# A hybrid mLSTM and convolution block on one core: four contraction tiles in a row for one PSUM bank, where each bank took one in turn

## The chip, the cores and the metric

The kernel runs on one core of one Trainium2 chip, as one launch. The metric is the device time of one execution in microseconds (us), shown as the median of the runs of a kernel. The engines are TensorE (PE; its weight loads are a row of their own, PEld), VectorE (DVE), ScalarE (ACT), GpSimd (POOL) and SyncE (SP), which issues the transfers.

## What is computed

One encoder layer on 2048 tokens of width 1024, in float32, followed by a final RMSNorm. Cut to what matters:

```
u    = rmsnorm(x, norm_g)
proj = u @ w_in                       # 1024 -> 5*1024 + 8 + 3*1024 columns
q, k, v, o_pre, z_m, i_pre, f_pre, glu_a, glu_g, z_c = split(proj)
hm   = mlstm_chunkwise(q, k, v, i_pre + b, f_pre + b)       # 4 heads of 256
hm   = headwise_rmsnorm(sigmoid(o_pre) * hm) * mh_norm_g * silu(z_m)
c    = causal_depthwise_conv31(glu_a * sigmoid(glu_g)) + conv_b
c    = silu(layernorm(c)) * silu(z_c)
h    = x + concat(hm, c) @ w_out                            # 2048 -> 1024 columns
out  = rmsnorm(h, final_norm_g)
```

## The kernel before

The tokens are taken in two halves of 1024. Every large product is made of three fp32r products: a float32 operand is split into a high part and the rest (`uh`, `ul` for activations, `wh`, `wl` for weights), and `wh*uh + wh*ul + wl*uh` is summed in PSUM.

The work is cut into units (`unit`, line 315). A unit fills four PSUM banks, `ps[0]` to `ps[3]` (tiles `gm_<n>_0` to `gm_<n>_3`; n is the number of the unit's first weight tile), from the pool `gm`, which has five banks. It runs over the contraction in steps `kc`: 8 steps of 128 rows in the input projection, 16 in the output projection. `products(kc, i)` (line 321) issues the matmuls of one step into one bank: three of 512 columns, or six of 256, or three of 264. Lines 350 to 357 hold the order: the step is the outer loop, the bank the inner one, so a bank takes one contraction tile and then its neighbour takes the same one. After the last step, lines 361 to 368 hand each bank to `evac`, which reads it out on ACT and DVE with high priority; the next unit needs those banks again.

The units of one half are, in order: one GLU unit (`g`), the two units of v of head 0 with the gates (`v0`), another `g`; then for each of the four heads v (head 0 had its own), o, z, q, k and two `g` units; at last four units `c`. Then the next half, then eight units of the output projection (blocks `b` of 512 tokens, `nn` of 512 columns).

Weights come as a stream. `w_load` (line 193) fetches two tiles (`wr`) in one transfer, `w_prep_` (line 210) splits a tile: ACT casts it to `wh` (line 215), POOL subtracts to get `wl` (line 216). The pool `wp` holds four tiles of each kind, and `w_advance(i)` (line 221) asks for tiles up to i + 3. A weight tile covers two steps in the input projection and one in the output projection.

Beside the units run three streams: the mLSTM of the head just projected, cut into slots, one slot after each step (`ml_slot`, line 173); the convolution's 31 taps for each channel block and the layer norm, taken from a queue at a fixed rate (`pump`, line 138), with most of the work on DVE; and the loads of the next activations (`hook`). For each chunk of 128 tokens the mLSTM runs `s0` (scores `sk` on PE; weighted scores `w`, their split `wsh`, `wsl`; scaled queries split into `qssh`, `qssl`), two slots later `s1` (`num` on PE, out of those splits and the split state `c0h`, `c0l`, `c1h`, `c1l`), and then the transposes `mt`. A tile scheduler orders each engine's instructions by priority, the place in the program, and its own timeline; the order is then fixed, and each engine works through its own list in that order.

Of the kernel before, what the change touches and what calls it, by code (L numbers as in the profile page):

```python
# [19 lines left out]
P = 128  # L20
D = 1024            # model width
SEQ = 2048
HT = 1024           # tokens per half
NH = 4              # mLSTM heads
HD = 256            # head width
L = 128             # mLSTM chunk
NCH = HT // L       # chunks per half
NB = 8              # 128-channel blocks of the conv group
# [3 lines left out]
VW = HD + 2         # value row with the ones column (even width)  # L32

# columns of the per-feature vector pack
# [5 lines left out]
def hybrid_block_kernel(  # L40
    ctx: ExitStack,
    tc: tile.TileContext,
    x: bass.AP,        # [SEQ, D]
    xT: bass.AP,       # [2, 8, P, HT]
    wu: bass.AP,       # [NU, 2, P, 4, 256]
    wv0: bass.AP,      # [2, P, 4, 264]
    wo: bass.AP,       # [2, 8, P, 2, 512]
    vecs: bass.AP,     # [P, NVEC]
    bg: bass.AP,       # [1, 8]
    fg: bass.AP,       # [1, D]  # L50
    out: bass.AP,      # [1, SEQ, D]
):
# [3 lines left out]
    WARM = 16  # L56

# [5 lines left out]
    wp = pool("wp", 4)  # L63
# [17 lines left out]
    ones = cp.tile([P, P], F32, name="ones")  # L81
    nc.gpsimd.memset(ones, 1.0)
    # until the data arrive: load the first function table, wake the tensor engine
# [48 lines left out]
    def in_turn(ins):  # L132
        """the first of the background work after a pause stays behind what was emitted before it"""
        if pin[0]:
            tc.keep_in_program_order(ins)
            pin[0] = False
# [19 lines left out]
    # mLSTM work in slots, one per step of the products that it runs beside  # L156
# [30 lines left out]
    # every entry: (dram AP of two tiles [P, 2, n], n); tiles are prepared ahead  # L187
# [31 lines left out]
    WAHEAD = 3  # L219

    def w_advance(i):
        """make tiles up to i + WAHEAD ready (emission order)"""
# [9 lines left out]
    uh, ul = {}, {}  # L232

    # The reciprocal rms of a token scales its row of every product, so the
    # products start on x * norm_g and the factor is applied where they leave PSUM.
# [19 lines left out]
    def bcast_cols(cols, n, nm):  # L255
        """[P tokens, n] columns -> PSUM [P, n*128]: the values along the free dim on all partitions"""
# [56 lines left out]
    wpos = [0]  # L313

    def unit(kind, nk, kpt, ncol, opnd, evac, step_us=2.6, hook=None, toks=None, ntail=0):
        """nk steps over the contraction, kpt per weight tile of kpt*ncol columns;
        the last ntail steps run bank by bank"""
# [31 lines left out]
        tail = nk - ntail  # L349
        for kc in range(tail):  # L350
            w_advance(base + kc // kpt)
            if hook is not None:
                hook(kc)
            for i in range(4):
                products(kc, i)
            ml_slot()
            pump(step_us * PUMP)
        for kc in range(tail, nk):
            w_advance(base + kc // kpt)
        wpos[0] += nk // kpt  # L360
        for i in range(4):
            for kc in range(tail, nk):
                products(kc, i)
            if hook is not None:
                for kc in range(tail + i * ntail // 4, tail + (i + 1) * ntail // 4):
                    hook(kc)
            with first_hand():
                evac(i, ps[i])
# [752 lines left out]
```

## Time and profile before

| | |
|---|---|
| runs (us) | 2030.17, 2029.78, 2030.05 |
| median (us) | 2030.05 |
| profiled execution, span from the first to the last instruction (us) | 2027.0 |
| PE busy | 1997.0 us (99%), 11562 matmuls |
| DVE busy | 1431.9 us (71%) |
| ACT busy | 828.6 us (41%) |
| POOL busy | 803.1 us (40%) |
| mean granted TensorE clock | 0.993 of 2.4 GHz |

The profiled execution is shown with its span alone; the times of the runs are 2.8 to 3.2 us above it, which is what lies around a span. A busy PE is not a PE at its peak: matmuls overlap in the records, so the pace is read from the distance between starts. The granted clock is one of two levels, 1.00 (2.4 GHz) and 0.50 (1.2 GHz); a stretch that holds both shows a mean.

### The profile page before, as it was taken

How to read it: one execution, taken by the hardware profiler on the slowest of the kernel's cores; microseconds unless marked ns; L12 is line 12 of the kernel's file. 1: busy time of each engine (PE TensorE's matmuls, PEld its weight loads, DVE VectorE, ACT ScalarE, POOL GpSimd, SP SyncE). 2: the span in 40 equal slices, each digit the busy share in tenths (PEclk: the TensorE clock that was granted, in tenths of full speed). 3: DMA queues.
4: the chain of work that ended last, by engine and by line, in shares of the span. 5: the costliest groups of instructions: out<-in, count | busy, mean ns of one | idle time of the engine just before them, and what ended most of it. 6: DMA issues, size and time to landing. Idle time of an engine off the chain costs nothing. (4 is left out here: it accounts for less than half of the span.)

```text
span 2027.0 us, 29786 instructions
## 1 busy us (share of the span) xinstructions
PE 1997.0 (99%) x11562; PEld 1750.5 (86%) x11562; DVE 1431.9 (71%) x1915; ACT 828.6 (41%) x1703; POOL 803.1 (40%) x740
## 2 busy tenths in 40 slices
PE   9999999999999999999999999999999999999998
PEld 7998898899899888888789879988998888788886
DVE  5598887689588855646799998977895658733231
ACT  5233432443343255535445225424523555543332
POOL 4632432343343232534333423433422326556464
PEclk9999999999999999999999999999999999999999
DMA  4121121111122233335311211211221566766452
GB/s 150 63 68 53 57 67 50 63 48 63 53 68 65 82 110 104 121 107 164 106 56 43 68 52 58 74 53 52 68 69 53 161 222 206 266 206 232 151 182 94
DMA packets 85837, 204.11 MB, mean 101 GB/s; under 512 B 7296, under 2 KB 40256, under 8 KB 85696
## 3 DMA queue, kind: packets, MB, share of 16 engines
q1 hardware_dynamic: 85696, 202.21, 29.8%
q8 instruction: 91, 1.49, 0.3%
q14 instruction: 50, 0.41, 0.1%
HBM read 159.15 MB, written 43.03 MB: 100 GB/s over the span
## 5 line engine op out<-in xcount | busy, mean ns | idle before, releaser
L216 POOL TENSOR_TENSOR wl<-wr,wh 128x512 fp32r<-128x512 f32 (+1 forms) x392 | 611.3, 1564 | 858.6 <-ACT wh L215 832.1
L781 DVE SCALAR_TENSOR_TENSOR y<-c,vec,y 128x1024 f32<-128x1024 f32 x480 | 707.3, 1474 | 9.5
L330 PE MATMUL gm<-ul_u,wh 128*128 128x512 f32 x1280 | 506.0, 395 | 0.4 <-DVE ul_u L287 0.4
L330 PE MATMUL gm<-uh_u,wl 128*128 128x512 f32 x1280 | 501.6, 394 | 0.0
L330 PE MATMUL gm<-uh_u,wh 128*128 128x512 f32 x1280 | 499.7, 395 | 1.6 <-DVE oz L445 1.0
L215 ACT CAST wh<-wr 128x512 fp32r<-128x512 f32 (+1 forms) x392 | 241.3, 619 | 596.5 <-PE gm L330 214.2
L337 PE MATMUL gm<-wh,uh_u 128*128 128x256 f32 x1408 | 286.9, 283 | 5.5 <-DVE oz L445 3.4
L330 PEld LDWEIGHTS gm<-uh_u,wh 128*128 128x128 f32 x1280 | 240.7, 188 | 54.5 <-DVE oz L445 1.4
L337 PE MATMUL gm<-wh,ul_u 128*128 128x256 f32 x1408 | 286.9, 282 | 0.0
L330 PEld LDWEIGHTS gm<-ul_u,wh 128*128 128x128 f32 x1280 | 241.0, 188 | 51.4 <-DVE ul_u L287 1.1
L330 PEld LDWEIGHTS gm<-uh_u,wl 128*128 128x128 f32 x1280 | 240.9, 188 | 51.6 <-POOL wl L216 0.3
L337 PE MATMUL gm<-wl,uh_u 128*128 128x256 f32 x1408 | 283.7, 282 | 0.0
L337 PEld LDWEIGHTS gm<-wh,uh_u 128*128 128x128 f32 x1408 | 219.2, 190 | 7.2 <-DVE oz L445 3.6
L337 PEld LDWEIGHTS gm<-wh,ul_u 128*128 128x128 f32 x1408 | 219.2, 190 | 0.1
L337 PEld LDWEIGHTS gm<-wl,uh_u 128*128 128x128 f32 x1408 | 217.8, 190 | 0.1
L344 PE MATMUL gm<-wh,uh_m 128*128 128x512 f32 x512 | 202.2, 396 | 2.2 <-ACT wh L215 2.2
L344 PE MATMUL gm<-wh,ul_m 128*128 128x512 f32 x512 | 202.6, 396 | 0.0
L344 PE MATMUL gm<-wl,uh_m 128*128 128x512 f32 x512 | 199.3, 396 | 0.8 <-POOL wl L216 0.8
L344 PEld LDWEIGHTS gm<-wh,uh_m 128*128 128x128 f32 x512 | 96.6, 189 | 24.7 <-ACT wh L215 2.5
L344 PEld LDWEIGHTS gm<-wl,uh_m 128*128 128x128 f32 x512 | 96.5, 188 | 23.2 <-POOL wl L216 1.2
L344 PEld LDWEIGHTS gm<-wh,ul_m 128*128 128x128 f32 x512 | 96.5, 189 | 22.2
L694 POOL TENSOR_TENSOR ss<-ss,nhalf 128x1 f32<-128x1 f32 x64 | 54.7, 854 | 133.3 <-ACT sq L693 131.0
(216 smaller groups left out, 2390.2 us busy)
## 6 DMA issues: line engine op xcount, KB each, us to landing
wr<-in_wu SPq DMA_DIRECT2D x123, 512.0 KB, 3.5
wr<-in_wo SPq DMA_DIRECT2D x64, 512.0 KB, 3.5
mr<-mixs SPq DMA_DIRECT2D x32, 512.0 KB, 4.6
ysc<-y SPq DMA_DIRECT2D x16, 512.0 KB, 2.6
mixs<-mo SPq DMA_DIRECT2D x32, 256.0 KB, 2.1
zsc<-zc SPq DMA_DIRECT2D x32, 256.0 KB, 2.2
ly<-ysc SPq DMA_DIRECT2D x16, 512.0 KB, 4.7
lz<-zsc SPq DMA_DIRECT2D x16, 512.0 KB, 5.7
```

What stands on the lines that cost most here:

```text
L215: nc.scalar.copy(hi[:, :n], s)
L216: nc.gpsimd.tensor_tensor(out=lo[:, :n], in0=s, in1=hi[:, :n].bitcast(F32), op=ALU.subtract)
L330: nc.tensor.matmul(ps[i], wt[:, o + cb * P : o + (cb + 1) * P], at[:, tb * 512 : (tb + 1) * 512], start=st, stop=sp_,)
L337: nc.tensor.matmul(ps[i][:, t2 * 256 : (t2 + 1) * 256], at[:, t * P : (t + 1) * P], wt[:, o : o + ncol], start=st and t2 == 0, stop=sp_, s ...
L344: nc.tensor.matmul(ps[i][:, :ncol], at[:, t * P : (t + 1) * P], wt[:, o : o + ncol], start=st, stop=sp_,)
L694: nc.gpsimd.tensor_tensor(out=ss, in0=ss, in1=nhalf[:, 0:1], op=ALU.pow)
L781: tc.keep_in_program_order(nc.vector.scalar_tensor_tensor(out=y, in0=c[:, j + i * H2 : j + (i + 1) * H2], scalar=col(V_CW, b * CW + j), in1=y,
```

## The change

`unit` gets a parameter `grp`. The steps are cut into groups of `grp`; within a group the bank is the outer loop and the step the inner one, so that one bank takes `grp` contraction tiles in a row before the next bank does. Input-projection units use 4, but the first and the last unit of each half keep 1; output-projection units use 2. In the last group each bank is read out as soon as its own products are issued. The mLSTM slots and the pumped work keep their rate, one per step's worth of products: with a group of four, one after each bank. All weight tiles of a group are asked for at its start, and stay in use until its last bank; the pool keeps its four buffers (`NW = 4`). Line numbers move by one or two. Comments are removed as well.

```diff
-    wp = pool("wp", 4)
+    wp = pool("wp", NW)
...
-    WAHEAD = 3
+    WAHEAD = NW - 1
...
-    def unit(kind, nk, kpt, ncol, opnd, evac, step_us=2.6, hook=None, toks=None, ntail=0):
+    def unit(kind, nk, kpt, ncol, opnd, evac, step_us=2.6, hook=None, toks=None, ntail=0, grp=1):
...
-        tail = nk - ntail
-        for kc in range(tail):
-            w_advance(base + kc // kpt)
-            if hook is not None:
-                hook(kc)
-            for i in range(4):
-                products(kc, i)
+        def step():
             ml_slot()
             pump(step_us * PUMP)
-        for kc in range(tail, nk):
-            w_advance(base + kc // kpt)
-        wpos[0] += nk // kpt
-        for i in range(4):
-            for kc in range(tail, nk):
-                products(kc, i)
...
-            with first_hand():
-                evac(i, ps[i])
-            for _ in range(ntail // 4):
-                ml_slot()
-                pump(step_us * PUMP)
+        bounds = list(range(0, nk - ntail, grp)) + [nk - ntail] + ([nk] if ntail else [])
+        for lo, hi in zip(bounds, bounds[1:]):
+            for kc in range(lo, hi):
+                w_advance(base + kc // kpt)
+            if hi == nk:
+                wpos[0] += nk // kpt
+            for i in range(4):
+                cut = lambda j: lo + j * (hi - lo) // 4
...
+                for kc in range(lo, hi):
+                    products(kc, i)
+                if hi == nk:
+                    with first_hand():
+                        evac(i, ps[i])
+                for _ in range(cut(i + 1) - cut(i)):
+                    step()
...
+            grp = 1 if ui in (0, len(s) - 1) else 4
...
-                unit("fm", 8, 2, 256, opnd, ev_glu(hf, i), hook=hook)
+                unit("fm", 8, 2, 256, opnd, ev_glu(hf, i), hook=hook, grp=grp)
...
-                 ntail=4 if (b, nn) == (3, 1) else 0)
+                 ntail=4 if (b, nn) == (3, 1) else 0, grp=2)
```

How PE's order moves, at three places. First, inside the unit of q of head 3 in the first half (`gm_108`; the rows name bank, activation part and weight part). Before:

```order
L330 MATMUL gm_108_1_6870<-uh_u0_5_238,wh110_6798 128x512
L330 MATMUL gm_108_1_6870<-ul_u0_5_239,wh110_6798 128x512
L330 MATMUL gm_108_1_6870<-uh_u0_5_238,wl110_6799 128x512
L330 MATMUL gm_108_2_6871<-uh_u0_5_238,wh110_6798 128x512
L330 MATMUL gm_108_2_6871<-ul_u0_5_239,wh110_6798 128x512
L330 MATMUL gm_108_2_6871<-uh_u0_5_238,wl110_6799 128x512
L330 MATMUL gm_108_3_6872<-uh_u0_5_238,wh110_6798 128x512
L330 MATMUL gm_108_3_6872<-ul_u0_5_239,wh110_6798 128x512
L330 MATMUL gm_108_3_6872<-uh_u0_5_238,wl110_6799 128x512
```

And on PE in the same unit of the changed kernel, its second group:

```order
L331 MATMUL gm_108_0_6870<-uh_u0_4_230,wh110_6749 128x512
L331 MATMUL gm_108_0_6870<-ul_u0_4_231,wh110_6749 128x512
L331 MATMUL gm_108_0_6870<-uh_u0_4_230,wl110_6750 128x512
L331 MATMUL gm_108_0_6870<-uh_u0_5_238,wh110_6749 128x512
L331 MATMUL gm_108_0_6870<-ul_u0_5_239,wh110_6749 128x512
L331 MATMUL gm_108_0_6870<-uh_u0_5_238,wl110_6750 128x512
L331 MATMUL gm_108_0_6870<-uh_u0_6_246,wh111_6874 128x512
L331 MATMUL gm_108_0_6870<-ul_u0_6_247,wh111_6874 128x512
L331 MATMUL gm_108_0_6870<-uh_u0_6_246,wl111_6875 128x512
L331 MATMUL gm_108_0_6870<-uh_u0_7_254,wh111_6874 128x512
L331 MATMUL gm_108_0_6870<-ul_u0_7_255,wh111_6874 128x512
L331 MATMUL gm_108_0_6870<-uh_u0_7_254,wl111_6875 128x512
```

The bank changed after three products and now changes after twelve. Over the program PE's list has 2629 such stretches on one `gm` bank before and 1365 after, with the same 11356 matmul instructions.

Second, PE in the unit of z of head 0 in the second half (`gm_152`), where its fourth bank is first written. Before:

```order
L337 MATMUL gm_152_2_9322<-wh155_9324,uh_u1_7_8280 128x256 x2
L337 MATMUL gm_152_2_9322<-wh155_9324,ul_u1_7_8281 128x256 x2
L337 MATMUL gm_152_2_9322<-wl155_9325,uh_u1_7_8280 128x256 x2
L337 MATMUL gm_152_3_9323<-wh152_9118,uh_u1_0_8102 128x256 x2
L337 MATMUL gm_152_3_9323<-wh152_9118,ul_u1_0_8103 128x256 x2
L337 MATMUL gm_152_3_9323<-wl152_9119,uh_u1_0_8102 128x256 x2
```

In the changed kernel PE stands thus at the same point:

```order
L338 MATMUL gm_152_2_9322<-wl153_9181,uh_u1_3_8178 128x256
L338 MATMUL gm_152_0_9320<-wh154_9186,uh_u1_4_8198 128x256 x2
L338 MATMUL gm_152_0_9320<-wh154_9186,ul_u1_4_8199 128x256
L338 MATMUL gm_152_3_9323<-wh152_9044,uh_u1_0_8102 128x256 x2
L338 MATMUL gm_152_3_9323<-wh152_9044,ul_u1_0_8103 128x256 x2
L338 MATMUL gm_152_3_9323<-wl152_9045,uh_u1_0_8102 128x256 x2
```

Before, the scheduler ran the first three banks through all eight steps and left the whole of the fourth bank for the end; now the fourth bank starts after the first group, with the first products of bank 0's second group ahead of it.

Third, PE at the first chunk of the mLSTM of head 1 in the second half, beside the GLU unit `gm_192`. Before:

```order
L330 MATMUL gm_192_3_11740<-uh_u1_3_8178,wh193_11654 128x512
L330 MATMUL gm_192_3_11740<-ul_u1_3_8179,wh193_11654 128x512
L595 MATMUL num_1_1_0_11811<-v_1_1_0_10937,wsh_1_1_0_11768 128x258 x2
L595 MATMUL kv_1_1_0_0_11821<-v_1_1_0_10937,kw_1_1_0_11765 128x258 x3
L595 MATMUL num_1_1_0_11811<-v_1_1_0_10937,wsl_1_1_0_11769 128x258
L330 MATMUL gm_192_3_11740<-uh_u1_3_8178,wl193_11655 128x512
```

In the changed kernel these rows of PE read:

```order
L331 MATMUL gm_192_1_11743<-ul_u1_7_8281,wh195_11746 128x512
L331 MATMUL gm_192_1_11743<-uh_u1_7_8280,wl195_11747 128x512
L596 MATMUL num_1_1_0_11816<-v_1_1_0_10782,wsh_1_1_0_11779 128x258 x2
L596 MATMUL kv_1_1_0_0_11826<-v_1_1_0_10782,kw_1_1_0_11776 128x258
L596 MATMUL num_1_1_0_11816<-v_1_1_0_10782,wsl_1_1_0_11780 128x258
```

The chunk's last `sk` row stands 26 rows of 512 columns above `num` before and 60 such rows above it now. For the first chunk of head 0 in that half it is 29 rows before and 62 now. For some later chunks it goes the other way: chunk 7 of head 1 in the first half has 29 rows between `sk` and `num` before and 16 now.

## Rows read from the trace of the kernel before

**Rows 1.** The page's head: the span, and busy time of each engine.
```profile
span 2027.0 us, 29786 instructions
...
PE 1997.0 (99%) x11562; PEld 1750.5 (86%) x11562; DVE 1431.9 (71%) x1915; ACT 828.6 (41%) x1703; POOL 803.1 (40%) x740
```

**Rows 2.** What PE waited for: us in total, times, longest us.
```profile
PE num L595 <- DVE qssl L586: 4.0, 3, 2.5
PE gm L337 <- DVE oz L445: 3.4, 1, 3.4
PE us L247 <- DVE sm L296: 2.8, 1, 2.8
PE gm L344 <- ACT wh L215: 2.2, 1, 2.2
PE num L595 <- ACT wsh L585: 2.1, 1, 2.1
PE mt L708 <- DVE hm L700: 1.6, 1, 1.6
...
PE gm L337 <- ACT oz L432: 1.2, 2, 0.9
PE gm L330 <- DVE oz L445: 1.0, 1, 1.0
PE gm L344 <- POOL wl L216: 0.8, 1, 0.8
PE gm L337 <- DVE v L402: 0.8, 1, 0.8
```

**Rows 3.** PE's timeline in unit gm_164: start, us, engine, line, operation, tiles.
```profile
1005.13 0.39 PE L330 MATMUL gm<-uh_u,wl 128*128 128x512 f32 x1
1005.36 0.39 PE L330 MATMUL gm<-uh_u,wh 128*128 128x512 f32 x1
1005.59 0.39 PE L330 MATMUL gm<-ul_u,wh 128*128 128x512 f32 x1
1005.82 0.39 PE L330 MATMUL gm<-uh_u,wl 128*128 128x512 f32 x1
1006.04 0.39 PE L330 MATMUL gm<-uh_u,wh 128*128 128x512 f32 x1
1006.27 0.39 PE L330 MATMUL gm<-ul_u,wh 128*128 128x512 f32 x1
1006.50 0.39 PE L330 MATMUL gm<-uh_u,wl 128*128 128x512 f32 x1
```

**Rows 4.** PE's timeline in unit gm_152, around its fourth bank's first product.
```profile
936.02 0.40 PE L337 MATMUL gm<-wl,uh_u 128*128 128x256 f32 x2
939.85 0.80 PE L337 MATMUL gm<-wh,uh_u 128*128 128x256 f32 x2 [3.43 <-DVE oz L445]
940.44 0.63 PE L337 MATMUL gm<-wh,ul_u 128*128 128x256 f32 x2
```

**Rows 5.** Stretches with PEclk (the granted clock) of about 0.50, and one on DVE's load.
```profile
core 0: us, PE busy (x) PEld busy (x) DVE busy (x) ACT busy (x) POOL busy (x), PEclk, DMA share, GB/s
...
938.50:945.30 6.80, 5.45 (x25) 5.46 (x26) 3.10 (x6) 1.65 (x5) 1.27 (x1) 0.50 0.67 225
1058.00:1061.40 3.40, 3.14 (x15) 2.75 (x14) 2.93 (x5) 1.35 (x5) 1.80 (x3) 0.50 0.57 170
1201.30:1204.70 3.40, 3.40 (x12) 2.91 (x13) 3.37 (x4) 0.41 (x1) 0.00 (x0) 0.51 0.44 154
1754.30:1757.70 3.40, 3.40 (x10) 2.61 (x9) 3.37 (x5) 0.00 (x0) 0.00 (x0) 0.50 0.86 309
...
1000.00:1210.00 210.00, 200.10 (x1224) 177.43 (x1223) 197.24 (x247) 75.06 (x169) 72.06 (x64) 0.98 0.17 57
```

**Rows 6.** PE's groups by shape: the first-chunk products of the second half.
```profile
L595 PE MATMUL num<-c0h_i,qssl 128*128 128x258 f32 x4 | 1.4, 346 | 3.8 <-DVE qssl L586 3.8
```

**Rows 7.** The page's groups: the two halves of a weight tile's preparation.
```profile
L216 POOL TENSOR_TENSOR wl<-wr,wh 128x512 fp32r<-128x512 f32 (+1 forms) x392 | 611.3, 1564 | 858.6 <-ACT wh L215 832.1
...
L215 ACT CAST wh<-wr 128x512 fp32r<-128x512 f32 (+1 forms) x392 | 241.3, 619 | 596.5 <-PE gm L330 214.2
```

**Rows 8.** ACT's timeline in the output projection, casts between layer-norm and activation work.
```profile
1740.96 2.08 ACT L875 ACTIVATE ly<-ly,vec 128x256 f32<-128x256 f32 x4 [2.42 <-DVE ly L870]
1742.95 0.60 ACT L215 CAST wh<-wr 128x512 fp32r<-128x512 f32 x1
1743.46 2.08 ACT L875 ACTIVATE ly<-ly,vec 128x256 f32<-128x256 f32 x4
...
1746.22 1.04 ACT L274 CAST uh_m<-mr 128x1024 fp32r<-128x1024 f32 x1
```

More of the change, by code (lines that the diff above doesn't have):

```diff
@@ L56, in hybrid_block_kernel @@
     WARM = 16
+    NW = 4
     def pool(name, bufs, **kw):
@@ L347, in products @@
                     )
-        tail = nk - ntail
-        for kc in range(tail):
-            w_advance(base + kc // kpt)
-            if hook is not None:
-                hook(kc)
-            for i in range(4):
-                products(kc, i)
+        def step():
             ml_slot()
             pump(step_us * PUMP)
-        for kc in range(tail, nk):
-            w_advance(base + kc // kpt)
-        wpos[0] += nk // kpt
-        for i in range(4):
-            for kc in range(tail, nk):
-                products(kc, i)
-            if hook is not None:
-                for kc in range(tail + i * ntail // 4, tail + (i + 1) * ntail // 4):
-                    hook(kc)
-            with first_hand():
-                evac(i, ps[i])
-            for _ in range(ntail // 4):
-                ml_slot()
-                pump(step_us * PUMP)
+        bounds = list(range(0, nk - ntail, grp)) + [nk - ntail] + ([nk] if ntail else [])
[6 more added lines that the diff above has]
+                cut = lambda j: lo + j * (hi - lo) // 4
+                if hook is not None:
+                    for kc in range(lo, hi) if hi - lo < 2 and i == 0 else range(cut(i), cut(i + 1)) if hi - lo > 1 else ():
+                        hook(kc)
+                for kc in range(lo, hi):
[5 more added lines that the diff above has]
+                    step()
     q_t, k_t, v_t, oz_t = {}, {}, {}, {}
@@ L972, in hybrid_block_kernel @@
             if nm == "g":
-                unit("fm", 8, 2, 256, opnd, ev_glu(hf, i), hook=hook)
+                unit("fm", 8, 2, 256, opnd, ev_glu(hf, i), hook=hook, grp=grp)
             elif nm == "c":
-                unit("fm", 8, 2, 256, opnd, ev_zc(hf, i), hook=hook)
+                unit("fm", 8, 2, 256, opnd, ev_zc(hf, i), hook=hook, grp=grp)
             elif nm == "q":
-                unit("fm", 8, 2, 256, opnd, ev_q(hf, i), hook=hook)
+                unit("fm", 8, 2, 256, opnd, ev_q(hf, i), hook=hook, grp=grp)
             elif nm == "k":
-                unit("fm", 8, 2, 256, opnd, ev_k(hf, i), hook=hook)
+                unit("fm", 8, 2, 256, opnd, ev_k(hf, i), hook=hook, grp=grp)
                 mlstm(hf, i)
             elif nm == "o":
-                unit("tm2", 8, 2, 256, opnd, ev_o(hf, i), hook=hook)
+                unit("tm2", 8, 2, 256, opnd, ev_o(hf, i), hook=hook, grp=grp)
             elif nm == "z":
-                unit("tm2", 8, 2, 256, opnd, ev_z(hf, i), hook=hook)
+                unit("tm2", 8, 2, 256, opnd, ev_z(hf, i), hook=hook, grp=grp)
             elif i > 0:
-                unit("tm2", 8, 2, 256, opnd, ev_v(hf, i), hook=hook)
+                unit("tm2", 8, 2, 256, opnd, ev_v(hf, i), hook=hook, grp=grp)
             else:
                 for g in range(2):
-                    unit("tm", 8, 2, 264, opnd, ev_v0(hf, g, gt), step_us=1.35, toks=[4 * g + i for i in range(4)])
+                    unit("tm", 8, 2, 264, opnd, ev_v0(hf, g, gt), step_us=1.35, toks=[4 * g + i for i in range(4)], grp=grp)
                 gq.append([0, gates(hf, gt)])
```

## The prediction

> **What bounds the kernel now.** I read the page's head first: PE is busy 1997.0 of 2027.0 us, no other engine over 71% [rows 1]. So the question is what PE waits for, and how fast it runs when it doesn't. The view of waits answers the first. In groups [rows 2]: PSUM banks not yet read out, 3.4 + 1.2 + 1.0 + 0.8 = 6.4 us; the mLSTM's inputs, 4.0 + 2.1 + 1.6 = 7.7; weight tiles, 2.2 + 0.8 = 3.0; the start of the program, 2.8 for `us`. Rows under 0.5 us are left out. The second is read from the timeline of a unit of 512-column products [rows 3]: starts lie 0.23 us apart. A wait has a second price: after four of them a stretch of 3.4 or 6.8 us runs at a granted clock of 0.50, the lower of its two levels, 1.2 GHz [rows 5]; work done there takes twice the time. Waits and low clock are all that this change can move, since the matmuls are the same 11356 instructions. That is some 25 us beyond the start, so a gain over 1.3% is out of reach.
>
> **Part 1, the bank order itself: 0.** In rows 3 the bank changes at each `uh_u,wh` row. The two distances that lead to such a row are 0.23 and 0.22 us, the four others 0.23. I take no difference. The rows are given to 0.01 us, so with 2629 - 1365 = 1264 fewer changes the bound is 12.6 us either way. The Trainium skill (TensorE: Matmul & The Clock Gate, section "A second HAM failure mode: psum-queue depth-cycling") reports a kernel that cycled through banks, idled a little between groups and lost clock by it; by that rule fewer changes would gain beyond my sum. The trace doesn't agree: even spacing, and 0.98 granted over 1000 to 1210 us, where rows 3 lie.
>
> **Part 2, PSUM banks: -3.4 and -1.5.** A unit needs four of five banks. Before, bank 0 of a unit ended three banks' products, 3 x 3 x 0.23 = 2.1 us, before the unit did, and the next unit's second bank asked for it 0.7 us after: 2.8 us to read it out. Now bank 0 ends 3 x 12 x 0.23 = 8.3 us before the unit's end and is asked for 2.8 us after: 11 us. The longest such wait, 3.4 us in `gm_152` [rows 2, 4], is less than the 8.3 us added, and the order shows the cause gone too: the fourth bank no longer stands behind all steps of the other three. I take all of it: -3.4. The other three rows add to 3.0. They lie mostly in the second half, where DVE is busy 197.24 of 210 us [rows 5], and there the changed order still puts the fourth bank of some units (`gm_148`, `gm_172`, `gm_176`) 15 to 21 us behind the first. Half of them: -1.5. Bounds 0 and -6.4.
>
> **Part 3, the clock after that wait: -2.7.** From 939.85, when PE resumed [rows 4], to 945.3 it ran at 0.50 [rows 5]: 5.45 us, half of it lost.
>
> **Part 4, the first chunks of the second half: -3.8 and -1.7.** `num` waits 3.8 us in all for `qssl` in the four first chunks there [rows 6]; the longest wait is 2.5 [rows 2]. Between `sk`, which starts that chain, and `num` there were 26 products in head 1, 26 x 0.23 = 6.0 us; now there are 60, 13.8 us. In head 0, 29 became 62. The added 7 us and more exceed the wait. With it goes the low clock at 1201.3, where 3.4 us at 0.51 lost 1.7 [rows 5]. Bound: 0, if DVE's list is as late by then as PE is.
>
> **Part 5, later chunks: +2.1.** Here `sk` and `num` move closer: counted from the order, at 0.23 us for 512 columns and half of that for 256, the work between them is under 5 us in 14 of 64 chunks, against 4 before, and in the case shown (29 rows, now 16) it fell from 5.2 to 3.7 us. Nothing else hides the chain over ACT and DVE there. The trace has one wait of this kind, 2.1 us for `wsh` [rows 2]; I take one more. Bounds: 0, and 14 x 1.5 = 21 us.
>
> **Part 6, weight tiles: +3.0.** A group holds its tiles longer with the same four buffers. In the output projection a step is 12 x 0.23 = 2.8 us. Before, a buffer freed after its step had to be full again three steps later, 8.3 us. Now the first of a pair is free 4.8 us into a group of 5.5 us and needed at 11.0: 6.2 us, and the second the same. Cast and subtraction take 0.62 + 1.56 = 2.2 us [rows 7]; the second of a pair queues on POOL and takes 3.0. The margin falls from 6.1 to some 3.1 us. ACT works in order, and two layer-norm groups of 2.08 with a cast of 1.04 between weights [rows 8] make 5.2 us: late by 2.1. Such places are few (two groups for each of four layer-norm blocks): at most 8 x 2.1 = 17. At least it is -3.0 - 1.7, if the present waits and the low clock at 1754.3 [rows 2, 5] go. I take the present 3.0 us once more, since the present wait is already of this kind. In the input projection a group lasts 11 us and 12.4 us are left to refill; I cost that at nothing, the cover being those 12.4 against 2.2 to 3.0.
>
> The work per slot of the mLSTM and of the pumped queue is unchanged, the first and last unit of each half keep their order, and PE's first 100 rows are the same: 0 for the start.
>
> **Sum.** -3.4 - 1.5 - 2.7 - 3.8 - 1.7 + 2.1 + 3.0 = -8.0 us, against the span of 2027.0: 2019.0. The median of the runs lies 3.05 us above that span, so **2022.0 us**.
>
> **Rivals.** *Nearly all waits go.* For it: slack of 11 us against waits of at most 3.4. Without parts 5 and 6 the sum is -13.1 (2017); if every wait after the start and the four low-clock stretches go, -(6.4 + 7.7 + 3.0 + 2.7 + 3 x 1.7) = -24.9, 2005. Against it: DVE's load from 1000 to 1210.
>
> *The waits only change place.* In that stretch DVE is 94% busy [rows 5]; if it is the bound there, PE freed at the banks waits at the next `num` instead. Then only parts 2 (first term) and 3 stay, -6.1, against +5.1: 2029, no change that a measurement can tell.
>
> *The weight ring becomes the bound in the output projection,* slower than before. Place: the 64 pairs of tiles. It decides when a refill takes over 6.2 us from the buffer's release, which needs about 3.2 us of lateness on ACT or POOL at every pair. At 0.4 us a pair that is 25.6; with the sum short of part 6, -11.0 + 25.6 = +14.6: 2044.7. For it: the margin is halved. Against: rows 8 show such lateness around a layer norm, while most of the output projection has none.
>
> *A long stay in one bank is paced differently,* at the bound of part 1: 2009 or 2035. That the change doesn't do what it says is ruled out by the order, where a bank takes twelve products in a row.
>
> **How the numbers follow.** A difference of 0.2%, 4.1 us, is about what a measurement of this kernel can tell from no change. Chances: the forecast 0.43 and nearly all waits gone 0.20, both faster; changed places 0.22, the same; the weight ring 0.10; a different pace 0.02 faster and 0.03 slower. Faster 0.65, same 0.22, slower 0.13. The range is 2008 to 2034: it leaves out the far end of the second case, some 0.08, and nearly all of the slower ones. Most of the chance has one sign, so no second range is given.
>
> **What would show it.** Right: no wait of a `gm` product for `oz` near 936, no stretch of low clock there nor at 1201, the `qssl` row of first chunks gone, 512-column starts still 0.23 apart. Part 5 shows as waits of `num` for `wsh`, part 6 as waits of `gm` for `wh` or `wl` after 1650. Wrong: starts 0.01 apart from before in a full-clock stretch, weight waits summing to over 10 us, or a sum of PE's waits as large as now.

## The result and the profile after

The changed kernel took 2045.77 us (median of 2044.97, 2045.44, 2046.1 and 2050.15) against 2029.91 us for the kernel before on the same chip: ratio 1.0086, interval 1.0072 to 1.01. It is slower by 16 us, where 2022.0 was forecast and the range ended at 2034. The profiled execution has a span of 2043.0 us, 16.0 above [rows 1].

The page's head of the changed kernel:

```profile
span 2043.0 us, 29825 instructions
...
PE 2000.2 (98%) x11562; PEld 1752.0 (86%) x11562; DVE 1438.4 (70%) x1915; ACT 851.4 (42%) x1719; POOL 807.9 (40%) x740
```

The matmuls are the same. ACT has 16 more instructions, all of them loads of a function table (83 against 67), and with them 20.5 us more work. What PE waited for, which answers to [rows 2] (us in total, times, longest us):

```profile
PE gm L331 <- POOL wl L217: 9.0, 1, 9.0
PE gm L338 <- ACT oz L433: 4.0, 1, 4.0
PE num L596 <- ACT wsh L586: 3.9, 2, 3.3
PE num L596 <- DVE qssl L587: 3.8, 3, 2.2
...
PE num L596 <- ACT qssh L586: 2.4, 4, 1.1
PE gm L345 <- POOL wl L217: 2.3, 2, 1.7
```

Part of the forecast can be seen to have come: the 3.4 us for `gm` behind `oz` L445 are gone, and so are the two shorter bank waits of the GLU unit and of v. In their place stands one wait of 9.0 us for a weight tile, in the input projection, and one of 4.0 for a bank. The stretches (columns as in [rows 5]):

```profile
936.00:945.30 9.30, 9.30 (x70) 8.83 (x69) 8.83 (x12) 7.37 (x13) 2.53 (x2) 1.00 1.02 326
966.00:986.00 20.00, 11.02 (x42) 8.25 (x41) 14.12 (x20) 9.24 (x17) 10.87 (x2) 0.74 0.39 129
1090.00:1110.00 20.00, 15.98 (x113) 15.78 (x113) 16.34 (x26) 9.07 (x21) 3.27 (x6) 0.83 0.12 41
1195.00:1215.00 20.00, 16.70 (x76) 13.89 (x75) 18.63 (x18) 4.18 (x8) 2.85 (x2) 0.91 0.17 53
1000.00:1210.00 210.00, 202.02 (x1222) 180.02 (x1220) 187.69 (x228) 81.50 (x177) 72.93 (x65) 0.98 0.20 65
```

From 936 to 945.3 us PE now works without a pause at a granted clock of 1.00, where it stood still and then ran at 0.50 [rows 4, 5]. From 966 to 986 it works 11.02 of 20 us at a mean of 0.74, from 1090 to 1110 at 0.83. At 1195 nothing was won.

**Where the 16 us are.** I take the start of a unit as its first product into bank 0, in PE's timeline of each trace (the order of PE's list tells which product is which), and compare it with the kernel before, in us:

| kernel (edit below) | first tap | 148 | 156 | 164 | 172 | 180 | 208 | 228 | 264 | span |
|---|---|---|---|---|---|---|---|---|---|---|
| changed | 940 | +0.3 | -5.9 | +5.5 | +3.5 | +8.8 | +7.2 | +5.4 | +14.1 | +16.0 |
| e2, output alone | 987 | -0.3 | -6.8 | -6.4 | +3.1 | +1.2 | +3.3 | +3.2 | +4.1 | +5.6 |
| e9, two units alone | 989 | +2.1 | -4.4 | -4.0 | +6.1 | +3.9 | +3.3 | +3.1 | +3.9 | +2.1 |
| e3, two tiles on DVE | 940 | -0.2 | -6.4 | -2.0 | -4.1 | -0.3 | -1.0 | -2.8 | +6.2 | +7.7 |
| e8, q changed back | 940 | -0.1 | -6.3 | +8.4 | +6.1 | +12.3 | +12.8 | +10.9 | +20.1 | +22.4 |
| e7b, no hold | 958 | +1.6 | +2.9 | -0.5 | -2.2 | -4.5 | -3.8 | -5.6 | +0.2 | +2.1 |
| e12, taps later | 1014 | +1.7 | -4.5 | -4.2 | +23.1 | +19.4 | +22.6 | +20.9 | +33.4 | +35.3 |
| e15, no groups, taps early | 929 | -1.9 | -8.0 | 0.0 | -0.9 | -2.5 | -1.0 | -1.1 | 0.0 | -0.2 |
| e16, the same with 6 taps | 930 | -1.8 | -8.0 | -5.8 | +2.4 | +1.6 | +2.4 | +2.3 | +2.2 | +2.9 |
| e17, the same with 4 taps | 930 | -1.8 | -8.0 | -7.7 | -0.5 | -1.2 | +1.3 | +1.2 | +2.2 | +1.9 |

The columns are units by their first weight tile (148 starts at 893 us before, 164 at 996, 180 at 1114, 228 at 1421, 264 at 1654); "first tap" is the start, in us, of the first convolution tap of the second half on DVE, and the last column is the span less 2027.0. In the changed kernel 5.9 us are won up to unit 156, 11.4 lost up to 164, 4.6 won up to 176 (+0.9 there), 7.9 lost up to 180, 3.4 won up to 228, 8.7 lost up to 264 and 1.9 to the end. The gains sum to 13.9, close to the 13.1 of the forecast's parts 2 to 4, though they are not the same ones; the losses sum to 29.9, where it had 5.1.

**The 9 us.** PE in the unit of k of head 0 (`gm_160`) and POOL beside it:

```profile
969.35 0.50 PE L331 MATMUL gm<-uh_u,wh 128*128 128x512 f32 x1
969.69 0.39 PE L331 MATMUL gm<-ul_u,wh 128*128 128x512 f32 x1
979.05 0.80 PE L331 MATMUL gm<-uh_u,wl 128*128 128x512 f32 x1 [8.98 <-POOL wl L217]
```

```profile
969.38 10.87 POOL L217 TENSOR_TENSOR wl<-wr,wh 128x512 fp32r<-128x512 f32 x2 [9.88 <-ACT wh L216]
```

The next view is that of the tile `wl` from 940 to 985 us, durations in ns, least, median and longest:

```profile
L217 POOL TENSOR_TENSOR wl<-wr,wh x6: 1284/1786/9622, 942.8 to 979.0; 128x512 fp32r<-128x512 f32 x6
```

One subtraction of a tile took 9.6 us, and it began only at 969.38. ACT's list shows why it began so late, DVE's why it lasted:

```profile
966.71 2.08 ACT L876 ACTIVATE ly<-ly,vec 128x256 f32<-128x256 f32 x4 [3.70 <-DVE ly L871]
968.69 0.60 ACT L216 CAST wh<-wr 128x512 fp32r<-128x512 f32 x1
969.20 2.07 ACT L876 ACTIVATE ly<-ly,vec 128x256 f32<-128x256 f32 x4
971.18 0.60 ACT L216 CAST wh<-wr 128x512 fp32r<-128x512 f32 x1
...
975.57 2.19 ACT L843 ACTIVATE lq<-ly 128x1024 f32<-128x1024 f32 x2 [3.51 <-DVE ly L839]
977.67 1.05 ACT L383 COPY q<-gm 128x512 f32<-128x512 f32 x2
```

```profile
940.48 0.80 DVE L772 TENSOR_SCALAR y<-c,vec 128x1024 f32<-128x1024 f32 x1
...
961.50 3.92 DVE L782 SCALAR_TENSOR_TENSOR y<-c,vec,y 128x1024 f32<-128x1024 f32 x3
...
965.47 2.34 DVE L871 TENSOR_TENSOR ly<-ly,lnr 128x1024 f32<-128x1024 f32 x2
...
969.49 1.20 DVE L882 TENSOR_TENSOR ly<-ly,lz 128x1024 f32<-128x1024 f32 x1
970.62 1.27 DVE L782 SCALAR_TENSOR_TENSOR y<-c,vec,y 128x1024 f32<-128x1024 f32 x1
...
973.03 1.27 DVE L782 SCALAR_TENSOR_TENSOR y<-c,vec,y 128x1024 f32<-128x1024 f32 x1
...
974.33 2.34 DVE L839 TENSOR_TENSOR ly<-ly,lnm 128x1024 f32<-128x1024 f32 x2
```

In the changed kernel DVE starts the convolution of the second half (`y<-c,vec`) at 940.48 us, and 12 of its taps run before the layer norm's third block (`ly<-ly,lnr`), which comes at 965.47. ACT takes its list in order: the casts of tiles 162 and 163 and the read-out of q's banks (L383) stand behind parts of that layer norm. PE's last read of the buffer that tile 162 fills ended at 964.90; the cast began 3.8 us later, and PE asked for the tile at 969.35, 4.4 us after that read. DVE in the kernel before has the layer norm ten microseconds earlier and the taps last:

```profile
954.93 1.20 DVE L870 TENSOR_TENSOR ly<-ly,lnr 128x1024 f32<-128x1024 f32 x1
...
987.33 1.80 DVE L771 TENSOR_SCALAR y<-c,vec 128x1024 f32<-128x1024 f32 x1
```

### The profile page after: what moved, and what is told of

The parts are those of the page before. It is cut to its first block, busy times and chain, and to the rows that moved or that the text cites. A ratio compares the mean times of both kernels' runs of the same rounds, so it can differ in the third digit from the quotient of the medians.

```text
span 2043.0 us, 29825 instructions
## 1 busy us (share of the span) xinstructions
PE 2000.2 (98%) x11562; PEld 1752.0 (86%) x11562; DVE 1438.4 (70%) x1915; ACT 851.4 (42%) x1719; POOL 807.9 (40%) x740
## 4 chain that ended last, share of the span: by engine, by line
PE 77%; DVE 11%; ACT 4%; issue 4%; POOL 2%; DMA 2%; SPq 0%; POOLq 0%; DVEq 0%; ACTq 0%
PE gm L331 34%; PE gm L338 20%; PE gm L345 16%; DVE y L782 5%; PE num L596 3%; PE kv L596 2%; POOL wl L217 1%; DMA ly<-ysc 1%; PE sk L622 1%; ACT L618 1%; DVE sm L297 1%; PE mt L709 0%; PE sk L626 0%; DVE qssl L587 0%; ACT L803 0%
## 5 line engine op out<-in xcount | busy, mean ns | idle before, releaser
L782 DVE SCALAR_TENSOR_TENSOR y<-c,vec,y 128x1024 f32<-128x1024 f32 x480 | 698.6, 1455 | 8.6
L338 PE MATMUL gm<-wl,uh_u 128*128 128x256 f32 x1408 | 288.4, 282 | 0.0
L345 PEld LDWEIGHTS gm<-wh,uh_m 128*128 128x128 f32 x512 | 96.2, 188 | 22.4
```

What stands on the lines that cost most here:

```text
L338: nc.tensor.matmul(ps[i][:, t2 * 256 : (t2 + 1) * 256], at[:, t * P : (t + 1) * P], wt[:, o : o + ncol], start=st and t2 == 0, stop=sp_, s ...
L345: nc.tensor.matmul(ps[i][:, :ncol], at[:, t * P : (t + 1) * P], wt[:, o : o + ncol], start=st, stop=sp_,)
L782: tc.keep_in_program_order(nc.vector.scalar_tensor_tensor(out=y, in0=c[:, j + i * H2 : j + (i + 1) * H2], scalar=col(V_CW, b * CW + j), in1=y,
```

## The experiments

The theories: **W**, a group of four holds two weight tiles to its last bank, so that a refill is late. **O**, the weight ring in the output projection (a rival of the prediction). **D**, DVE is the bound in the second half up to about 1270 us, and waits of PE only change place there (also a rival of the prediction). **S**, a change of the plan shifts small waits about, whatever it is for. **P**, formed after ten runs: the new plan put taps ahead of the layer norm on DVE, and ACT's list carries the delay to PE. Ratios are to the kernel before on the same chip, with their interval.

**e1 and e2: one part of the change alone.**

```diff
-ntail=4 if (b, nn) == (3, 1) else 0, grp=2)
+ntail=4 if (b, nn) == (3, 1) else 0, grp=1)
```
```diff
-            grp = 1 if ui in (0, len(s) - 1) else 4
+            grp = 1
```

> Input projection in groups of four as in the changed kernel, output projection back to one step per bank. Theory W (one late weight tile in the input projection: a group of four holds both its tiles until its last bank, the list of PE runs on with bank 0 of the next group, so that a refill has some 3 us instead of the 12.4 us that the prediction took, and the subtraction of that tile on POOL then took 9.6 us beside the work of DVE): the loss stays, 2043 to 2047 us, with a wait of PE for wl of 8 to 10 us near 970. Rival O (the weight ring in the output projection, the rival of the prediction): back to 2028 to 2032 us.

> Output projection in groups of two as in the changed kernel, input projection back to one step per bank. Theory W: 2027 to 2033 us, since the part after 1650 us came out only about 1 us later in the changed kernel. Rival O: 2040 to 2047 us.

e1: 2044.91 us, 1.0079 (1.0064 to 1.0094), with the same 9.0 us for `wl`. e2: 2035.84 us, 1.0032 (1.002 to 1.0043), just beyond what was expected. O falls: the loss is in the input projection. But e2 shows something else. With one step per bank it has neither the wait near 936 nor its low clock (-6.8 at unit 156), and it pays that back at 1040 with one wait (PE's waits from 900 to 1260 us):

```profile
PE num L596 <- ACT wsh L586: 6.2, 2, 5.5
```

In its program that unit differs from the kernel before only at its end: a bank is read out before the next one's last products, and the last slot and the pumped work follow the read-outs. So the gain near 936 isn't owed to the groups.

**e3: two tiles subtracted on DVE.**

```diff
-        nc.gpsimd.tensor_tensor(out=lo[:, :n], in0=s, in1=hi[:, :n].bitcast(F32), op=ALU.subtract)
+        (nc.vector if i in (162, 163) else nc.gpsimd).tensor_tensor(out=lo[:, :n], in0=s, in1=hi[:, :n].bitcast(F32), op=ALU.subtract)
```

> The changed kernel with the subtraction of two weight tiles alone (162 and 163, the second group of k of head 0 in the second half) on DVE instead of POOL; outside that place the lists of the engines stay as they were. Theory W with POOL held up beside DVE as its main part: the wait of 9.0 us falls to at most 2.5 us, the 10.2 us of half clock after it shrink to at most 3.4, and the time falls by 9 to 13 us, to 2033 to 2037 us. Theory W without that part (the buffer comes free late and the cast is late, whichever engine subtracts): the wait stays over 6 us, 2042 to 2047 us. Rival D (DVE is the bound there, the waits only change place): the wait comes back within the next 50 us as waits for DVE, 2041 to 2046 us.

2038.05 us, 1.0045 (1.003 to 1.006), just outside what W expected; the span is 8.3 us below that of the changed kernel. The wait for `wl` is gone; PE then waited 2.1 us for the next thing on ACT's list, q's banks, and then worked 3.4 us at half clock:

```profile
PE gm L338 <- ACT oz L433: 4.2, 1, 4.2
PE num L596 <- ACT wsh L586: 3.9, 2, 3.3
PE gm L331 <- ACT q L383: 2.1, 1, 2.1
```

The step from unit 160 to 164 falls from 12.2 to 5.3 us. Not all of the 6.9 us between them are POOL's slow subtraction: the edit moved DVE's list too. Nine taps instead of 12 now stand ahead of the layer norm, and ACT comes to the layer norm and to the cast of tile 162 four us earlier (at 968.69 in the changed kernel):

```profile
962.63 2.08 ACT L876 ACTIVATE ly<-ly,vec 128x256 f32<-128x256 f32 x4 [0.15 <-DVE ly L871]
964.62 0.61 ACT L216 CAST wh<-wr 128x512 fp32r<-128x512 f32 x1
```

How much is due to each wasn't separated.

**e5: groups of two in the input projection,** one weight tile to a group.

```diff
-            grp = 1 if ui in (0, len(s) - 1) else 4
+            grp = 1 if ui in (0, len(s) - 1) else 2
```

> Groups of two in the input projection, so one weight tile for each group, held for as long as in the kernel before; output projection in groups of two as changed. Theory W (the hold of two tiles is what made the refill late): no wait for wl over 2 us between 930 and 1000, and 2026 to 2036 us. Rival D: the wait for banks near 1095 (4.2 us and half clock after it, 7.9 us in all) stays whatever the group, 2034 to 2040 us. Rival S (a change of the plan shifts small waits about at random): waits at places that neither kernel had, anywhere from 2025 to 2045 us.

2049.99 us, 1.0103 (1.0086 to 1.012): worse than groups of four, and above the ranges of all three theories. The taps start at 991, and there is no loss near 970 (0.4 us from unit 160 to 164). No wait for `wl` near 970, as W said, but 5.2 us for `wsh` at 1044 with 10.2 us of half clock, and more later. W accounts for one wait, not for the time.

**e6a and e6b: DVE relieved.** Every second tap of the second half is left out, in both kernels, so that their output is a different one.

```diff
-            push(1.15, tap(j))
+            push(1.15, tap(j) if hf == 0 or j % 2 else lambda: None)
```

> The kernel before with every second tap of the convolution left out in the second half of the tokens (120 of 240; their place in the queue of pumped work stays empty), so that DVE has about 120 x 1.2 = 144 us less to do there. Theory D (from 1000 to 1260 us DVE is the bound, and PE's waits there are what DVE's lateness leaves): the waits of PE for inputs of the mLSTM and for PSUM banks between 1000 and 1260 (some 9 us, with 6.8 us of half clock) go, 2012 to 2022 us. Rival S (waits come from how the plan falls, not from DVE's load): 2025 to 2035 us, with waits of a similar sum at other places.

> The changed kernel with the same taps left out. Theory D: the waits after 1000 us go here too, the late weight tile near 970 shrinks since POOL is held up less, and the changed order is no longer the slower one: 2010 to 2022 us, within 4 us of the kernel before without those taps, either side. Theory W alone (the weight tile held by a group, whatever DVE does): some 10 us behind the kernel before without those taps. Rival S: about 16 us behind it, or anything from 5 to 20.

Before without those taps: 2021.24 us, 0.9965 (0.9954 to 0.9977). Changed without them: 2019.32, 0.9958 (0.9943 to 0.9972). The 16 us are gone; the 1.9 us between the two lie within the intervals. PE's waits from 900 to 1260 us, first the kernel before without the taps, then the changed one:

```profile
PE gm L337 <- DVE v L402: 3.7, 1, 3.7
PE gm L337 <- DVE oz L445: 3.4, 1, 3.4
```
```profile
PE gm L331 <- ACT q L383: 5.0, 1, 5.0
```

And the stretch from 1000 to 1210, in the same order:

```profile
1000.00:1210.00 210.00, 203.72 (x1259) 182.75 (x1258) 134.04 (x213) 80.97 (x183) 64.47 (x68) 0.98 0.17 55
```
```profile
1000.00:1210.00 210.00, 209.45 (x1293) 186.93 (x1292) 132.03 (x210) 81.89 (x187) 67.37 (x70) 1.00 0.20 65
```

With DVE busy 132 of 210 us instead of 188, the groups do what parts 2 and 4 said: PE works 209.45 of 210 us at full clock. D holds for that stretch, as far as one edit that also makes a new plan can show it. The 5.0 us near 970 stay, since this plan too has the taps early (941).

**e7a and e7b: the pumped work isn't held for the gates,** so that the layer norm starts earlier.

```diff
-        hold[0] = 10**6
+        hold[0] = 10**6 if hf == 0 else 0
```

> The kernel before, but the pumped work of the second half no longer waits for the gates, so that the layer norm of the first half starts at about 820 us instead of 890 and fills DVE's idle time there (busy 19 of 50 us from 850 to 900). Theory D: DVE comes to the stretch from 1000 us with less left over, and the waits there shrink, 2018 to 2028 us. Rival S: 2025 to 2040 us. Against both: the gates themselves come later, and the first chunk with them, which costs up to 10 us.

> The changed kernel with the same edit. Theory D: 2020 to 2032 us, no more than 6 us behind the kernel before with the edit, and the subtraction on POOL near 970 no longer over 3 us, since the layer norm that held it up is done by then. Theory W without POOL's hold-up: the wait for the weight tile stays, 2038 to 2047 us.

Before with the edit: 2030.4, 1.0014 (1.0005 to 1.0024). Changed with it: 2030.51, 1.001 (1.0 to 1.0019). The first is above D's range and within S's, the second within D's. One line that has nothing to do with groups takes 15 us from the changed kernel (1.0086 to 1.001), and then there is no difference between the two orders.

**e8 and e9: q changed back alone, and two units changed alone.**

```diff
+            grp = 1 if ui in (0, len(s) - 1) or (hf, ui) == (1, 5) else 4
```
```diff
+            grp = 4 if (hf, ui) in ((1, 5), (1, 6)) else 1
```

> The changed kernel with one unit of 62 changed back: q of head 0 in the second half takes one step per bank again, so that its third weight tile comes free 5.5 us before the unit ends and not at its end. In the list of ACT the cast of tile 162 moves ahead of the two layer-norm groups that it stood behind; PE's run on bank 0 of the next unit stays. Theory W (the hold by a group makes the tile late): the wait of 9.1 us for wl near 970 is gone (under 1 us); what is left there is the wait for q's banks, 2 to 5 us, since ACT reads them out behind the layer norm; 2032 to 2039 us. Rival (only POOL's hold-up beside DVE matters, the release of the buffer does not): the wait stays over 6 us, 2042 to 2047 us.

> Groups of four in two units alone, q and k of head 0 in the second half; all others, the output projection too, take one step per bank. Theory W: a wait for wl of 2 to 9 us near 970 that the version without groups in the input projection did not have (its step there was within 0.5 us of the kernel before), so 2032 to 2042 us. Theory S (where DVE is the bound the plan moves waits about whatever the change): the wait at 970 may come, but the stretch up to 1110 us gives most of it back, and the time is that of the version without groups in the input projection, 2033 to 2038 us.

e8 missed: 2051.47, 1.0121 (1.0107 to 1.0136). The cast of tile 162 moved ahead as meant, and PE then stood at tile 163:

```profile
PE gm L331 <- POOL wl L217: 5.7, 1, 5.7
...
PE gm L331 <- ACT q L383: 3.4, 1, 3.4
PE gm L331 <- ACT wh L216: 1.6, 1, 1.6
```

The reason is in the lists: the cast of tile 163 still stands behind the layer norm (at 971.41), and as the plan finds no other bank free, bank 0 of `gm_160` takes all 24 products of the contraction before bank 1 gets its first (9 in the kernel before). One bank alone runs through four tiles in 24 x 0.23 = 5.5 us. Holding a tile for less only moved the wait by one tile. e9: 2031.21, 1.002 (1.0011 to 1.0029), below the ranges of both theories, with the groups in just those two units, no wait near 970, and 5.1 us for `wsh` at 1040 as in e2. W as a cause by itself falls. A deeper ring wasn't tried: with five buffers of each kind the kernel's tiles don't fit into SBUF.

**e10 and e14: a plan that falls a little differently,** in the changed kernel and in the kernel before.

```diff
-    PUMP = 0.5
+    PUMP = 0.51
```

> The changed kernel with the rate of the pumped work at 0.51 instead of 0.50: nothing that bears on groups, banks or weight tiles, only a plan that falls a little differently. Theory S: the wait of 9 us does not come back in its size, and the time is anywhere from 2028 to 2048 us; if it is below 2040, the size of the loss is one plan's luck. Theory W: 2042 to 2048 us, with a wait for wl of over 6 us between 950 and 1000.

> The kernel before with the rate of the pumped work at 0.51 instead of 0.50. If a small shift of the plan alone moves this kernel: 2031 to 2040 us, and the changed kernel's place behind it is smaller than it looks. If the kernel before is robust to it: 2026 to 2031 us.

e10: 2043.34, 1.008 (1.0066 to 1.0095), the wait of 9 us unchanged, in a plan with the taps at the same place. e14: 2036.61, 1.0046 (1.0029 to 1.0062): the kernel before loses 9 us by the same touch. So S doesn't hold for the 9 us, but a difference of a few us between two versions of this kernel can be the plan's alone.

**e12 and e15: the place of the taps, with groups and without.** e12 lets the first block's taps enter the queue later in the changed kernel; e15 puts twelve of them (the first and the eleven after it) ahead of the end of the layer norm's third block in the kernel before.

```diff
-        push(0.6, tap0)
+        push(30.6, lambda: None) if (hf, b) == (1, 0) else push(0.6, lambda: None); push(0.0, tap0)
```
```diff
-        push(0.6, tap0)
-        for j in range(1, CW):
-            push(1.15, tap(j))
+        taps = [(0.6, tap0)] + [(1.15, tap(j)) for j in range(1, CW)]
+        for it in taps: bgq.insert(len(bgq) - 17, it) if (hf, b) == (1, 0) and it in taps[:12] else bgq.append(it)
```

> The changed kernel with one thing moved: the taps of the second half's first convolution block enter the queue of pumped work 30 us of work later, so that on DVE they stand behind the layer norm's last block, as in the kernel before. Groups, banks and tiles stay. Theory P (the loss near 970 us is taps that the new plan put ahead of the layer norm on DVE; ACT's list, in order, then delays the cast of a weight tile and the read-out of q's banks): no wait for wl and none over 2 us for q's banks between 950 and 1000, the layer norm's silu at about 956 to 959 us as before instead of 967, 2028 to 2037 us. Theory W (the hold by a group): the wait for wl stays over 4 us, 2041 to 2047 us. Rival D in its strict form (DVE is the bound, whatever is saved near 970 is waited for later): the 5 us wait for wsh near 1040 and the half clock after it, as in the versions without groups in the input projection, and 2033 to 2042 us.

> The kernel before, no groups, with eleven taps of the second half's first convolution block put into the queue ahead of the end of the layer norm's third block, which is where the changed kernel's plan has them. Theory P: the layer norm's silu comes 8 to 12 us later, PE waits near 970 for a weight tile or for q's banks by 3 to 9 us with half clock after it, and 2033 to 2044 us without any group. Theory W or D: PE still gets its tiles one step at a time, no wait over 2 us there, 2026 to 2032 us.

e15: 2029.16, 1.001 (1.0001 to 1.0019). The time is below P's range and in that of W and D, but the wait is P's: without any group PE waits near 970, for q's banks. The layer norm and the read-out of q are late by the same ten microseconds. The casts of tiles 162 and 163 stand ahead of the layer norm here (960.40 and 965.05), and so PE doesn't wait for a tile:

```profile
PE gm L330 <- ACT q L382: 5.1, 1, 5.1
```
```profile
966.98 4.05 ACT L875 ACTIVATE ly<-ly,vec 128x256 f32<-128x256 f32 x8
...
973.46 2.19 ACT L842 ACTIVATE lq<-ly 128x1024 f32<-128x1024 f32 x2 [2.16 <-DVE ly L838]
975.65 1.07 ACT L382 COPY q<-gm 128x512 f32<-128x512 f32 x2
```

From unit 156 to 164 it loses 8.1 us, where the changed kernel loses 11.4: the taps make the loss, and the groups, which put the two casts behind the layer norm, add to it. The total stays, because the 6.2 us won near 936, and 1.9 before, pay for it. e12: with the taps behind the layer norm the groups cost nothing near 970 (-4.5 at unit 156, -4.2 at 164). P is shown for that place, from both sides. But the time became 2063.46, 1.0176 (1.0161 to 1.0191), above the ranges of all three theories. The taps then start at 1014, DVE is busy 42.2 of the 45 us from 1035 to 1080, and PE waits for what DVE and ACT make (900 to 1260 us):

```profile
PE num L596 <- ACT wsh L586: 13.0, 4, 6.9
PE num L596 <- DVE wsl L587: 2.6, 1, 2.6
```

Why it loses 28.9 us from unit 168 to 172, where e2 and e9 lose 11.1 and 11.7, stays open, as does why the plan moved the taps.

**e16 and e17: six or four early taps,** no groups.

> The kernel before, no groups, with 6 taps of the second half's first convolution block ahead of the end of the layer norm's third block, where the version with 11 had a wait of 5.3 us at 971 us and 1.1 near 1053, and the versions with none 5.2 to 7.0 us at 1040. Theory P with a middle: silu at about 961 to 963 us, the wait at 971 under 1.5 us, the one near 1040 under 4 us, the wait of 3.6 us at 936 gone: 2020 to 2027 us, below the kernel before. Strict D (a fixed sum): the two waits sum to 5 to 7 us and the time is 2027 to 2032 us.

> The same with 4 taps. Theory P with a middle: no wait at 971 us, 3 to 6 us near 1040, 2022 to 2029 us. Strict D: 2027 to 2033 us.

e16: 2033.64, 1.0031 (1.002 to 1.0042), above both ranges. e17: 2031.28, 1.0018 (1.0009 to 1.0026), within D's. (The views have the waits that the expectation calls 5.3 and 3.6 us as 5.1 and 3.4.) With 4, 6 and 12 early taps, the step from unit 160 to 164 loses 0.4, 1.9 and 8.1 us: the loss near 970 grows with the taps. With four, PE waits 7 us between 1035 and 1060 instead, and 8.8 us are lost from unit 168 to 172. There is no middle: what is saved near 970 is paid after 1035, as D in its strict form says, though e16's sum is above what D forecast. Both also run bank 0 of `gm_160` through all 24 products, as e15 does. So that run doesn't come from the groups, and alone it costs next to nothing (0.4 us in e17).

**e11 and e13: versions meant to beat both.** e11 is e7b, e13 is e12, each with one step per bank in the output projection and in the last five units of the second half.

```diff
+            grp = 1 if ui in (0, len(s) - 1) or hf == 1 and ui > len(s) - 6 else 4
```

> A version meant to beat both: the changed kernel with the pumped work of the second half not held for the gates, one step per bank in the output projection, and one step per bank in the last five units of the second half, where the groups bring chunks of the mLSTM closer to their inputs (4.9 us in the changed kernel). Theory D with part 5 of the prediction: 2030.5 - 0.9 - 4 = 2024 to 2028 us, 1 to 4 us below the kernel before. Theory S: 2027 to 2035 us.

> The version before this one, with one step per bank in the output projection and in the last five units of the second half. Theory P with part 5 of the prediction: 3 to 5 us below the version before this one, 2024 to 2032 us. Theory S: no such difference, within 2 us of it.

e11: 2027.51, 0.9999 (0.999 to 1.0009), within D's range but no difference to the kernel before. e13: 2054.49, 1.0135 (1.012 to 1.015), 9 below e12 and far above its range. No version found beats the kernel before.

## Why the prediction was wrong, point by point

**The step that failed** is the end of part 6: "In the input projection a group lasts 11 us and 12.4 us are left to refill; I cost that at nothing, the cover being those 12.4 against 2.2 to 3.0." Both sides of that comparison failed. The 12.4 us hold when four banks take turns. Where the other banks aren't free, one bank runs through four tiles in 5.5 us, and PE asked for tile 162 only 4.4 us after its buffer came free. Even 4.4 us would have covered a refill of 3.0: in e12 it is 4.0, without a wait. But the refill took 14.1 us: 3.8 until ACT, behind the layer norm, began the cast, 0.6 for the cast and 9.6 for the subtraction. The term measured 9.0 us of waiting and, with the work at half clock after it and small gaps, 12.2 us from unit 160 to 164, instead of nothing. Behind it lies a step that wasn't taken at all: the prediction looked at how the change moves PE's list, and not at DVE's, where the new plan had put 12 taps of other work ahead of a layer norm. e15, e16, e17 and e12 show that those taps, and not the groups, decide whether there is a loss at that place. That is the largest loss; the two next ones, 8.7 and 7.9 us below, stay without a shown cause.

*Part 1* was right: 0. Starts in the unit of the GLU at 1012 us, all in one bank, where [rows 3] change the bank after every three rows:

```profile
1012.47 0.40 PE L331 MATMUL gm<-uh_u,wh 128*128 128x512 f32 x1
1012.70 0.39 PE L331 MATMUL gm<-ul_u,wh 128*128 128x512 f32 x1
1012.93 0.39 PE L331 MATMUL gm<-uh_u,wl 128*128 128x512 f32 x1
1013.15 0.39 PE L331 MATMUL gm<-uh_u,wh 128*128 128x512 f32 x1
```

Over all neighbouring 512-column products of these units with starts under 0.3 us apart, the mean distance is 0.231 us in both kernels, and within 0.001 of that whether the bank changes (1070 times before, 380 now) or not.

*Parts 2 and 3* were right in size near 936 (-6.1 forecast, 6.2 won from unit 148 to 156), but the groups weren't needed for it: e2, e9 and e15 win as much, 6.2 to 6.5, with one step per bank in that unit, since its fourth bank no longer stands last there either. Of the prediction's two reasons the fourth bank was enough, and the slack of a group wasn't tested. The rest of part 2 turned round: a bank wait of 4.0 us at 1095, with 6.8 us at half clock, 7.9 in all. One of ACT's table loads, 1.28 us, lies inside that wait. The wait is in e1, e3, e8 and e10 too (4.0 to 4.2), all with the taps from about 940 us on. But e6b, with every second tap left out, doesn't have it, and e7a, without groups and with the taps from 960, has one of 3.3. It wasn't tried alone, and its cause stays open.

*Part 4* failed: the longest `qssl` wait (2.5) gave way to one for `wsh` (3.3), and the granted clock of 0.91 from 1195 to 1215 shows the low stretch still there. Its bound, "0, if DVE's list is as late by then as PE is", is what happened: DVE ran taps without a pause ahead of the weighted scores `w`, although PE's list had put more work before `num`.

```profile
1199.62 11.05 DVE L782 SCALAR_TENSOR_TENSOR y<-c,vec,y 128x1024 f32<-128x1024 f32 x7
1210.59 0.35 DVE L628 SCALAR_TENSOR_TENSOR w<-sk,rs,ee 128x128 f32<-128x128 f32 x1
```

*Part 5* was mis-sized, and its mechanism isn't shown: 2.1 forecast, 8.7 lost from unit 228 to 264, of which `num` waits for `qssl` and `qssh` are 4.3 (3.0 + 1.3; 0 before). The prediction counted chunks with under 5 us of work between `sk` and `num`. The three longest of these waits (2.2, 1.1 and 0.8) lie in chunks that have 6.2, 6.1 and 5.6 us there, where the kernel before had 6.9, 7.0 and 5.6. The other 4.4 us weren't traced. The part also misread its example: at its own price the work there fell from 6.4 to 3.5 us, and not from 5.2 to 3.7. Versions with groups in those units lose 4.5 to 12.5 us (2.4 with taps left out), those without at most 1.2; ungrouping the last five units didn't cure it (5.1 in e11, 9.0 in e13). *The output projection's half of part 6* was small, as forecast: 2.3 us of waits for `wl`, where the kernel before had 3.0 for its weights, and e1's ratio, without it, is only 0.0007 lower.

Of the rivals, "the waits only change place" was the nearest: its mechanism is shown by e6, e16 and e17 for the stretch after 1000 us, but its price of 2029 left out that a moved wait can be longer than the one it replaces and brings its own half clock. The rival on the other side put the ring's trouble in the output projection, where nothing happened.

## What to carry to other kernels

A change of order in a planned program is a change of every engine's list. Before costing it, compare the lists of all engines around the places where one of them is the bound, and look for background work that moved ahead of something on the path; here a neutral touch of the plan alone was worth up to 9 us. A cover counted from tile to tile holds only as long as all the banks that share the tiles are free and the engines that refill a tile come to it at once. And where another engine is the bound, a wait taken away from PE is no gain until that engine has less to do: the same change was 16 us slower with DVE full, and level with the kernel before once DVE was relieved.

## What the runs showed of the hardware

A subtraction of 128x512 on POOL, 1.28 us at the shortest in that view, took 9.6 us at 969, and 6.35 in e8, while DVE worked through operations with two tiles as inputs, almost without a pause. Of the 392 in the changed kernel all others took at most 2.9 us; the kernel before had one of 6.2, beside five such operations in a row. Where no DVE instruction stood beside it (93 of the 392), it took at most 1.34. With these subtractions on DVE and the layer norm earlier, PE didn't wait for the two tiles (e3). The Trainium skill (SBUF — State Buffer, section "Who interferes with whom") states that a DVE instruction with two SBUF inputs and a POOL instruction that reads SBUF block each other, the second until the first is done. The trace agrees: 76 of the 392 took 2.0 to 2.5 us, about one tap longer than the shortest, all of them beside such an operation, and of the 480 taps 80 took over 2 us, all beside work on POOL, where the 283 without it took at most 1.29. And it shows more: at 969 POOL ended only after the next instructions as well, seven large ones in a row, 1.1 us after the last.

The stretches of granted clock 0.50 (1.2 GHz) were longer than the 3.4 and 6.8 us of [rows 5]: 10.2 us from 972.3 about the 9 us wait, 13.7 in e8 from 974.9, and 17.1 in e12 from 1061.5. The part that lies in the wait itself costs nothing more. In the changed kernel PE resumed at 979.05, 3.4 us before the stretch ended, and lost 1.7 us; after the wait at 1095, it worked 6 of 6.8 us at half clock and lost 3. A moved wait is dearer than its length by half of the time for which PE then works at the lower clock.
